# Wider temporaries, an A step's normalisation on ScalarE, and its scores as one scheduling group, in a two-layer hybrid encoder

## The chip, the cores and the metric

The kernel runs on one core of one Trainium2 chip. The metric is the device time of one execution in microseconds (us). A core has a matmul engine (TensorE, written PE, with its weight loads as PEld), a vector engine (VectorE, DVE), an activation engine (ScalarE, ACT), GpSimd (POOL) and a sync engine (SP), which here only issues transfers. Each runs its own instruction list in order, and semaphores tie the lists together. Operands lie in SBUF, an on-chip memory of 128 partitions; matmul results lie in PSUM.

## The reference

Two layers on 512 tokens of width 1024, in float32. Each layer is:

```
h = RMSNorm(x); proj = h @ w_in                      # 2304 columns: qa ka va qb kb vb
qa, ka, qb, kb: per-head RMSNorm, then rotary
group A (8 q heads, 2 kv heads, dim 64, window +-128, learned sink logit per head):
  scores = qa . ka / 8, masked;  m = max(max(scores), sink);  p = exp(scores - m)
  p = p / (sum(p) + exp(sink - m));                  ya = p @ va
group B (4 heads, two q/k halves, values of dim 128):
  w = softmax(s0) - lam * softmax(s1);               yb = rmsnorm(w @ vb) * (1 - lam0)
x = x + concat(ya, yb) @ w_out
h = RMSNorm(x); gate, val = split(h @ w_up)          # 2 x 2816 columns
x = x + (silu(conv3(gate)) * val) @ w_down
```

The change touches group A's line `p = p / (...)`, the moment at which its `scores` are made, and where the tiles lie in SBUF. What is computed stays the same.

## The kernel before, in words

**Matmuls.** Float32 accuracy comes from a split: each operand is a high part (rounded to the matmul's own 32-bit format) and a low part (what is left), and one product is three matmuls (`mm3`, L198 to L200: high·high, high·low, low·high). The second operand of a call, `b` in `mm3`, is the one that streams through the array (the moving operand); the first is loaded as weights. Weights arrive by DMA in units of `wr`; ACT makes the high part `wh` (L185), and DVE or, for the B projections and the output projection, POOL makes the low part `wl` (L186).

**Stages of a layer.** (1) Projection of A's k, v and q (`akv`, `aq0`, `aq1`), the hidden state as weights and 256 weight columns as moving operand. (2) A woven region: attention on one track and, on the other, B's projections (`bv`, `bq`, `bk`, twice) and then the output projection (`wo`). Attention is eight A steps (four query blocks for each of two head pairs, `ip`) and then the B steps. (3) The tail of the output projection. (4) The channel mixer in two parts: `up` (in all 704 triples of 128x512 matmuls with the normed hidden state `nf_h`/`nf_l` moving) and `dn` (352 triples with `act`, the gated activation, moving).

**An A step.** `a_scores` makes the scores of two head groups in a two-bank PSUM tile `sc_a` (L425), adds the mask and takes the maxima on DVE (L429, into `so_a` and `mx_a`), and does this a second time for the other two heads. Small DVE operations on 128x4 tiles follow (L438 to L442), four exponentials on ACT with row sums (L447), a sum and a reciprocal on DVE (L450, L452), and four multiplications of a 128x256 or 128x384 tile by the reciprocal of its row (L454, on DVE). In the next step's turn `a_values` transposes the four tiles on PE (`pt_a`, L470), splits them into high and low parts `p_a` on ACT and DVE (L251, L252) and multiplies by the values (`pv_a`).

**Order.** The two tracks are generators. `weave` always advances the track that is behind in the weights its steps yield. That sets the order in which the code is written out, and thereby the priority of each instruction; a list scheduler with a model of the engines' times then makes each engine's list, and picks by priority among what its model says is ready. Code under `tc.high_priority()` gets priorities as if it stood at the program's start.

**Where tiles lie.** A pool lays its tiles one behind the other in each partition, each rounded up to 32 bytes. Of the eight `tmp` slots each is as long as its longest tile, the 514 floats of `gp` (2056 bytes, rounded to 2080, which is 32 over a multiple of 64). `cols`, `rows` and three one-float constants also add odd multiples of 32. As a sum of these, the tiles of the tags `keep`, `pair`, `prob` and `rp` start 32 bytes past a multiple of 64: among them `act`, the output projection's `y`, `p_a`, A's and B's k and q. The tiles of `hid` (`nf_h`, `nf_l` and the hidden state of the projections), `wr`, `wh`, `wl` and `x` start at a multiple of 64.

Of the kernel before, what the change touches and what calls it, by code (L numbers as in the profile page):

```python
# [21 lines left out]
DEPTH = 2  # L22
HD = 64
# [14 lines left out]
N_COL = NK + NK + 3 * NF + NF + 1  # L38
N_ROW = 4 * HD + 8 + 4 * HD
# [3 lines left out]
def kernel(  # L43
# [16 lines left out]
    nc = tc.nc  # L60
    PSUM = bass.MemoryType.PSUM

    const = ctx.enter_context(tc.tile_pool(name="const", bufs=1))
    sb = ctx.enter_context(tc.tile_pool(name="sb", bufs=1))
# [12 lines left out]
        return sb.tile([P, 2, S], F32R, tag="prob", bufs=4, name=name)  # L77

    def tmp(name, n=S):
        return sb.tile([P, n], F32, tag="tmp", bufs=8, name=name)  # L80

    def rp(name):
        return sb.tile([P, 2, CW], F32, tag="rp", bufs=RP, name=name)
# [1 line left out]
    def small(name, n):  # L85
        return sb.tile([P, n], F32, tag="small", bufs=28, name=name)
# [10 lines left out]
    def sc2(name):  # L97
        return ps.tile([P, 2, S], F32, tag="sc", bufs=1, name=name)
# [40 lines left out]
    x_v = xT.rearrange("(k p) s -> p k s", p=P)  # L139
    out_v = out.rearrange("(k p) s -> p k s", p=P)  # L140
    ident = const.tile([P, P], F32, name="ident")
    cols = const.tile([P, DEPTH, N_COL], F32, name="cols")
    rope_sb = const.tile([P, 2, NT, HD], F32, name="rope_sb")
    mask_sb = const.tile([P, 3 * P], F32, name="mask_sb")
    ones = const.tile([P, 1], F32, name="ones")
    nhalf = const.tile([P, 1], F32, name="nhalf")
    nc.gpsimd.memset(ones, 1.0)
    nc.gpsimd.memset(nhalf, -0.5)

# [53 lines left out]
    class Norm:  # L203
# [47 lines left out]
        nc.scalar.copy(hi, src)  # L251
        nc.vector.tensor_tensor(out=lo, in0=src, in1=hi, op=ALU.subtract)  # L252

    warm = const.tile([P, 1], F32, name="warm")
    nc.scalar.activation(warm, ones, AF.Copy, scale=ones)
    nc.sync.dma_start(cols, col_par)
    nc.sync.dma_start(x_sb[0], x_v[:, 0])
    emit_unit()
    for k in range(1, NK):
# [12 lines left out]
    for l in range(depth):  # L272
        lam_init = 0.8 - 0.6 * math.exp(-0.3 * l)

        rows = sb.tile([P, N_ROW], F32, tag="rows", bufs=1, name=f"rows{l}")
        nc.sync.dma_start(rows, row_par[l:l + 1, :].partition_broadcast(P))
        tabs = [None] * 4

# [13 lines left out]
        if l:  # L292
# [14 lines left out]
                                op0=ALU.subtract, op1=ALU.subtract)  # L307
# [103 lines left out]
        def a_scores(ip, qb):  # L411
            kb0, kb1 = max(qb - 1, 0), min(qb + 2, NT)
            n = (kb1 - kb0) * P
            m0 = (kb0 - qb + 1) * P
            nm = f"a{l}_{ip}_{qb}"
            q, k = qa[ip], ka
            mx = small(f"mx_{nm}", 4)
            so = []
            for i in range(2):
                scp = sc2(f"sc_{nm}_{i}")  # L420
                sc = (scp[:, 0], scp[:, 1])
                for j, (u, v) in enumerate(((0, 0), (0, 1), (1, 0))):
                    for g in range(2):
                        rs = slice(g * HD, (g + 1) * HD)
                        nc.tensor.matmul(sc[g][:, :n], lhsT=q[u][rs, i, qb * P:(qb + 1) * P],  # L425
                                         rhs=k[v][rs, kb0 * P:kb1 * P], start=j == 0, stop=j == 2)
                for g in range(2):
                    s = tmp(f"so_{nm}_{i}_{g}")
                    nc.vector.tensor_tensor_reduce(out=s[:, :n], in0=sc[g][:, :n], in1=mask_sb[:, m0:m0 + n],  # L429
                                                   op0=ALU.add, op1=ALU.max, scale=1.0, scalar=-3.0e38,  # L430
                                                   accum_out=mx[:, 2 * i + g:2 * i + g + 1])
                    so.append(s)
                yield 1.0
            by_g = lambda v: v.rearrange("p (g i) -> p i g", g=2)[:, 2 * ip:2 * ip + 2, :]
            pairs = lambda v: v.rearrange("p (i g) -> p i g", g=2)
            rq = rqa[:, qb, 2 * ip:2 * ip + 2, :]
            ngm = small(f"ng_{nm}", 4)
            nc.vector.tensor_tensor(out=pairs(mx), in0=pairs(mx), in1=rq, op=ALU.mult)  # L438
            nc.vector.scalar_tensor_tensor(out=pairs(ngm), in0=pairs(mx), scalar=-1.0, in1=by_g(nsink),
                                           op0=ALU.mult, op1=ALU.min)  # L440
            dn = small(f"dn_{nm}", 4)
            nc.vector.tensor_tensor(out=pairs(dn), in0=pairs(ngm), in1=by_g(sink), op=ALU.add)  # L442
            es = small(f"es_{nm}", 4)
            nc.scalar.activation(es, dn, AF.Exp)
            ls = small(f"ls_{nm}", 4)
            for i in range(4):
                nc.scalar.activation(so[i][:, :n], so[i][:, :n], AF.Exp, bias=ngm[:, i:i + 1],  # L447
                                     scale=rqa[:, qb, 2 * ip + i // 2, i % 2:i % 2 + 1],
                                     accum_out=ls[:, i:i + 1])
            nc.vector.tensor_tensor(out=ls, in0=ls, in1=es, op=ALU.add)  # L450
            rl = small(f"rl_{nm}", 4)
            nc.vector.reciprocal(rl, ls)  # L452
            for i in range(4):
                nc.vector.tensor_scalar(out=so[i][:, :n], in0=so[i][:, :n], scalar1=rl[:, i:i + 1], scalar2=None,  # L454
                                        op0=ALU.mult)
            a_so[ip, qb] = so

        def a_values(ip, qb):
# [134 lines left out]
        def attend():  # L593
# [104 lines left out]
        for pi, (f0, f1) in enumerate(FF_PARTS):  # L698
            act = []
            for f in range(f0, f1):  # L700
# [7 lines left out]
                g = tmp(f"gp{l}_{f}", S + 2)  # L708
# [103 lines left out]
```

## Time and profile before

| | |
|---|---|
| median of 3 runs (lowest to highest) | 1294.73 us (1293.69 to 1295.14) |
| the profiled execution: its time | 1294.65 us |
| its span on the core | 1292.9 us |
| mean granted TensorE clock | 0.977 of full speed |
| PE busy in the span | 1239.9 us (96%) |
| DVE, ACT, POOL busy | 754.8, 541.8, 359.6 us |
| woven region's A part, layer 0 and layer 1 | about 65 to 190 us and 690 to 820 us |
| woven region's later part | about 190 to 300 us and 820 to 935 us |

The page shows one execution. A line of its table of groups gives, for all instructions of one line of code, engine and operation: output and inputs, their shapes, how often, the busy time, the mean duration in ns, and the idle time of the engine ahead of them with what ended most of it. A timeline row gives start and length in us, engine, line, operation and, in brackets, how long the engine had stood idle and who ended that. A row of the table of windows gives, for a stretch, its length, each engine's busy time with the number of instructions, the granted clock, the DMA share and GB/s. In the profile a matmul's duration is longer than its distance to the next one, because matmuls overlap: the rate is read from one start to the next. The mask operation at L429 is shown under its custom name.

### The profile page before, as it was taken

How to read it: one execution, taken by the hardware profiler on the slowest of the kernel's cores; microseconds unless marked ns; L12 is line 12 of the kernel's file. 1: busy time of each engine (PE TensorE's matmuls, PEld its weight loads, DVE VectorE, ACT ScalarE, POOL GpSimd, SP SyncE). 2: the span in 40 equal slices, each digit the busy share in tenths (PEclk: the TensorE clock that was granted, in tenths of full speed). 3: DMA queues.
4: the chain of work that ended last, by engine and by line, in shares of the span. 5: the costliest groups of instructions: out<-in, count | busy, mean ns of one | idle time of the engine just before them, and what ended most of it. 6: DMA issues, size and time to landing. Idle time of an engine off the chain costs nothing. (4 is left out here: it accounts for less than half of the span.)

```text
span 1292.9 us, 17021 instructions
## 1 busy us (share of the span) xinstructions
PE 1239.9 (96%) x6648; PEld 1040.6 (80%) x6648; DVE 754.8 (58%) x1245; ACT 541.8 (42%) x943; POOL 359.6 (28%) x354
## 2 busy tenths in 40 slices
PE   6999997989999999999999999888999999999998
PEld 6988885778888888888899889766888888888886
DVE  6678787766755334554446778756765542355532
ACT  4455564435433213333345666444443331233321
POOL 5746283114111000112247556602321110011100
PEclk8999999899999999999999999969999999999999
DMA  5312121013332333332332111201233323333232
GB/s 174 99 34 66 42 65 34 26 40 103 96 96 87 96 94 114 97 93 72 98 98 81 51 36 64 65 1 34 65 99 113 96 76 98 106 98 98 80 108 90
DMA packets 32625, 102.93 MB, mean 80 GB/s; under 512 B 3616, under 2 KB 4000, under 8 KB 32544
## 3 DMA queue, kind: packets, MB, share of 16 engines
q1 hardware_dynamic: 32544, 101.84, 25.9%
q8 instruction: 52, 0.85, 0.3%
q14 instruction: 29, 0.24, 0.1%
HBM read 99.73 MB, written 2.10 MB: 79 GB/s over the span
## 5 line engine op out<-in xcount | busy, mean ns | idle before, releaser
L185 ACT CAST wh<-wr 128x1024 fp32r<-128x1024 f32 (+3 forms) x210 | 197.5, 944 | 408.6 <-PE up L199 171.0
L199 PE MATMUL up<-nf_l,wh 128*128 128x512 f32 x704 | 274.7, 390 | 0.6 <-DVE nf_l L217 0.5
L200 PE MATMUL up<-nf_h,wl 128*128 128x512 f32 x704 | 274.1, 390 | 0.4
L198 PE MATMUL up<-nf_h,wh 128*128 128x512 f32 x704 | 273.4, 390 | 0.0
L186 DVE TENSOR_TENSOR wl<-wr,wh 128x1024 fp32r<-128x1024 f32 (+3 forms) x174 | 192.5, 1110 | 108.7 <-ACT wh L185 108.4
L718 POOL TENSOR_TENSOR cv<-cv,rb 128x512 f32<-128x512 f32 x44 | 59.2, 1346 | 519.3 <-ACT cv L717 519.3
L199 PEld LDWEIGHTS up<-nf_l,wh 128*128 128x128 f32 x704 | 132.2, 188 | 29.8 <-DVE nf_l L217 2.8
L200 PEld LDWEIGHTS up<-nf_h,wl 128*128 128x128 f32 x704 | 132.2, 188 | 28.8 <-DVE wl L186 1.5
L198 PEld LDWEIGHTS up<-nf_h,wh 128*128 128x128 f32 x704 | 132.2, 188 | 27.5 <-ACT nf_h L216 0.2
L200 PE MATMUL dn<-act,wl 128*128 128x512 f32 x352 | 139.5, 397 | 0.0
L199 PE MATMUL dn<-act,wh 128*128 128x512 f32 x352 | 139.4, 397 | 0.0
L198 PE MATMUL dn<-act,wh 128*128 128x512 f32 x352 | 138.8, 395 | 0.0
L186 POOL TENSOR_TENSOR wl<-wr,wh 128x1024 fp32r<-128x1024 f32 x36 | 86.9, 2419 | 106.4 <-ACT wh L185 106.4
L711 DVE TENSOR_TENSOR gp<-up,rb 128x512 f32<-128x512 f32 x44 | 30.3, 693 | 103.4 <-PE up L200 98.4
L199 PEld LDWEIGHTS dn<-act,wh 128*128 128x128 f32 x352 | 66.8, 190 | 16.5
L198 PEld LDWEIGHTS dn<-act,wh 128*128 128x128 f32 x352 | 66.0, 188 | 16.5
L200 PEld LDWEIGHTS dn<-act,wl 128*128 128x128 f32 x352 | 66.1, 188 | 15.5
L719 DVE TENSOR_TENSOR cv<-cv,up 128x512 f32<-128x512 f32 x44 | 30.2, 687 | 81.8 <-POOL cv L718 72.1
L522 ACT ACTIVATE e_b<-sc_b,mx_b,rqb 128x512 f32<-128x512 f32 x64 | 49.2, 773 | 49.5 <-DVE mx_b L519 45.6
L732 DVE TENSOR_TENSOR x<-x,dn 128x512 f32<-128x512 f32 x32 | 22.0, 689 | 79.7 <-PE dn L200 79.7
L717 ACT ACTIVATE cv<-cv 128x512 f32<-128x512 f32 x44 | 27.7, 631 | 71.6 <-DVE cv L716 71.5
L518 DVE TENSOR_REDUCE mx_b<-sc_b 128x2 f32<-128x1024 f32 x32 | 39.0, 1219 | 7.9 <-PE sc_b L516 7.8
(212 smaller groups left out, 2559.9 us busy)
## 6 DMA issues: line engine op xcount, KB each, us to landing
wr<-w_up SPq DMA_DIRECT2D x88, 512.0 KB, 3.6
wr<-w_in SPq DMA_DIRECT2D x36, 512.0 KB, 3.6
wr<-w_down SPq DMA_DIRECT2D x32, 384.0 KB, 3.0
wr<-w_down SPq DMA_DIRECT2D x32, 320.0 KB, 2.9
wr<-w_out SPq DMA_DIRECT2D x16, 512.0 KB, 3.6
x<-xT SPq DMA_DIRECT2D x8, 256.0 KB, 5.3
outT<-x SPq DMA_DIRECT2D x8, 256.0 KB, 2.0
rows<-row_par SPq DMA_DIRECT2D x2, 260.0 KB, 4.2
```

The lines of the kernel that those rows point to most:

```text
L185: nc.scalar.copy(hi[:, o], raw[:, o])
L186: eng.tensor_tensor(out=lo[:, o], in0=raw[:, o], in1=hi[:, o], op=ALU.subtract)
L198: nc.tensor.matmul(acc, lhsT=a[0], rhs=b[0], start=start, stop=False)
L199: nc.tensor.matmul(acc, lhsT=a[0], rhs=b[1], start=False, stop=False)
L200: nc.tensor.matmul(acc, lhsT=a[1], rhs=b[0], start=False, stop=stop)
L518: nc.vector.tensor_reduce(out=mx, in_=scp, axis=AX, op=ALU.max)
L522: nc.scalar.activation(e[c], sc[c], AF.Exp, bias=mx[:, c:c + 1], scale=rq[:, c:c + 1], accum_out=lsum[:, c:c + 1])
L711: nc.vector.tensor_tensor(out=g[:, 1:S + 1], in0=acc[0], in1=rb, op=ALU.mult)
L717: nc.scalar.activation(cv, cv, AF.Silu)
L718: nc.gpsimd.tensor_tensor(out=cv, in0=cv, in1=rb, op=ALU.mult)
L719: nc.vector.tensor_tensor(out=cv, in0=cv, in1=acc[1], op=ALU.mult)
L732: nc.vector.tensor_tensor(out=x_sb[d], in0=x_sb[d], in1=acc, op=ALU.add)
```

## The change

It has three parts.

1. Tiles are made wider: a `tmp` tile has 528 floats and is used through a view of its first columns; `cols` and `rows` get 7 and 8 spare columns; the three one-float constants become columns of one 16-float tile. All tiles but the `small` and `smp` ones then start at a multiple of 64 bytes. The DMA into `cols` now writes two stretches of 105 floats in each partition, where it was one of 210.
2. The 64 multiplications at L454 (four in each of 16 A steps) move from DVE to ACT, as an activation `Copy` with the reciprocal as scale.
3. The two halves of an A step's scores (12 matmuls) and their four mask-and-maximum operations stand under `tc.high_priority()`, and the generator yields once, 2.0, instead of twice 1.0.

```diff
     def tmp(name, n=S):
-        return sb.tile([P, n], F32, tag="tmp", bufs=8, name=name)
+        return sb.tile([P, S + 16], F32, tag="tmp", bufs=8, name=name)[:, :n]
...
-    cols = const.tile([P, DEPTH, N_COL], F32, name="cols")
+    cols = const.tile([P, DEPTH, N_COL + 7], F32, name="cols")
...
-    ones = const.tile([P, 1], F32, name="ones")
-    nhalf = const.tile([P, 1], F32, name="nhalf")
+    unit = const.tile([P, 16], F32, name="unit")
+    ones, nhalf, warm = (unit[:, i:i + 1] for i in range(3))
...
-    warm = const.tile([P, 1], F32, name="warm")
     nc.scalar.activation(warm, ones, AF.Copy, scale=ones)
-    nc.sync.dma_start(cols, col_par)
+    nc.sync.dma_start(cols[:, :, :N_COL], col_par)
...
-        rows = sb.tile([P, N_ROW], F32, tag="rows", bufs=1, name=f"rows{l}")
+        rows = sb.tile([P, N_ROW + 8], F32, tag="rows", bufs=1, name=f"rows{l}")[:, :N_ROW]
...
-            for i in range(2):
-                scp = sc2(f"sc_{nm}_{i}")
...
-                yield 1.0
+            with tc.high_priority():
+                for i in range(2):
+                    scp = sc2(f"sc_{nm}_{i}")
...
+            yield 2.0
...
             for i in range(4):
-                nc.vector.tensor_scalar(out=so[i][:, :n], in0=so[i][:, :n], scalar1=rl[:, i:i + 1], scalar2=None,
-                                        op0=ALU.mult)
+                nc.scalar.activation(so[i][:, :n], so[i][:, :n], AF.Copy, scale=rl[:, i:i + 1])
             a_so[ip, qb] = so
```

Past L254 the lines of the changed kernel have numbers smaller by one up to the A step's scores; L454 is L454 in both. The order of SP's list is the same in both. PE's list differs only in the A parts of the two woven regions and just ahead of them; the lists of the B steps, the output projection and the channel mixer have the same order.

On DVE, in layer 0, between the reciprocal of one A step (`rl_a_0_2`, head pair 0, query block 2) and the split of its last transposed block (`p_a_0_1_2` is the step before), the list before is this (the last numbers of a name are buffer numbers):

```order
L450 TENSOR_TENSOR ls_a_0_2_940<-ls_a_0_2_940,es_a_0_2_938 128x4
L452 RECIPROCAL rl_a_0_2_946<-ls_a_0_2_940 128x4
L429 ISA so_a_0_3_0_0_1052,mx_a_0_3_1044<-sc_a_0_3_0_1045,mask_sb 128x256
L429 ISA mx_a_0_3_1044 128x1
L429 ISA so_a_0_3_0_1_1054,mx_a_0_3_1044<-sc_a_0_3_0_1045,mask_sb 128x256
L429 ISA mx_a_0_3_1044 128x1
L454 TENSOR_SCALAR so_a_0_2_0_0_906<-so_a_0_2_0_0_906,rl_a_0_2_946 128x384
L454 TENSOR_SCALAR so_a_0_2_0_1_908<-so_a_0_2_0_1_908,rl_a_0_2_946 128x384
L454 TENSOR_SCALAR so_a_0_2_1_0_929<-so_a_0_2_1_0_929,rl_a_0_2_946 128x384
L454 TENSOR_SCALAR so_a_0_2_1_1_931<-so_a_0_2_1_1_931,rl_a_0_2_946 128x384
L252 TENSOR_TENSOR p_a_0_1_2_991<-pt_a_0_1_2_986,p_a_0_1_2_991 128x512
```

and now this:

```order
L450 TENSOR_TENSOR ls_a_0_2_938<-ls_a_0_2_938,es_a_0_2_936 128x4
L452 RECIPROCAL rl_a_0_2_944<-ls_a_0_2_938 128x4
L429 ISA so_a_0_3_0_0_1050,mx_a_0_3_1042<-sc_a_0_3_0_1043,mask_sb 128x256
L429 ISA mx_a_0_3_1042 128x1
L429 ISA so_a_0_3_0_1_1052,mx_a_0_3_1042<-sc_a_0_3_0_1043,mask_sb 128x256
L429 ISA mx_a_0_3_1042 128x1
L252 TENSOR_TENSOR p_a_0_1_2_989<-pt_a_0_1_2_984,p_a_0_1_2_989 128x512
L429 ISA so_a_0_3_1_0_1061,mx_a_0_3_1042<-sc_a_0_3_1_1054,mask_sb 128x256
```

The four multiplications are gone from DVE's list, and the split follows the masks at once.

On ACT at the same place, between the last exponential of that step and the projection's scaled copy `raw_bq`, before:

```order
L447 ACTIVATE so_a_0_2_1_1_931,ls_a_0_2_940<-so_a_0_2_1_1_931,ng_a_0_2_933,rqa_377 128x384
L251 CAST p_a_0_1_2_991<-pt_a_0_1_2_986 128x512
L185 CAST wh_995<-wr_994 128x1024
L185 CAST wh_1001<-wr_1000 128x1024
L333 ACTIVATE raw_bq_1_1230<-pj_bq_1_1148,na_r 128x256 x2
```

and now:

```order
L447 ACTIVATE so_a_0_2_1_1_917,ls_a_0_2_938<-so_a_0_2_1_1_917,ng_a_0_2_931,rqa_375 128x384
L251 CAST p_a_0_1_2_989<-pt_a_0_1_2_984 128x512
L185 CAST wh_993<-wr_992 128x1024
L454 ACTIVATE so_a_0_2_0_0_904<-so_a_0_2_0_0_904,rl_a_0_2_944 128x384
L454 ACTIVATE so_a_0_2_0_1_906<-so_a_0_2_0_1_906,rl_a_0_2_944 128x384
L454 ACTIVATE so_a_0_2_1_0_915<-so_a_0_2_1_0_915,rl_a_0_2_944 128x384
L454 ACTIVATE so_a_0_2_1_1_917<-so_a_0_2_1_1_917,rl_a_0_2_944 128x384
L185 CAST wh_999<-wr_998 128x1024
L332 ACTIVATE raw_bq_1_1239<-pj_bq_1_1146,na_r 128x256 x2
```

The four multiplications stand behind one conversion of weights `wh` and ahead of the next.

On PE, at the start of layer 1's A part (the last bank of the projection `aq1`, whose transposes are `tr_qa_1`, and the first A step's scores), before:

```order
L371 MATMUL tr_qa_1_6027<-ident,raw_qa_1_6013 128x128 x4
L198 MATMUL pj_aq_1_6116<-wh_5883,na_h_5617 128x256
L199 MATMUL pj_aq_1_6116<-wl_5884,na_h_5617 128x256
L200 MATMUL pj_aq_1_6116<-wh_5883,na_l_5618 128x256
L198 MATMUL pj_aq_1_6116<-wh_5883,na_h_5668 128x256
L199 MATMUL pj_aq_1_6116<-wl_5884,na_h_5668 128x256
L200 MATMUL pj_aq_1_6116<-wh_5883,na_l_5669 128x256
L425 MATMUL sc_a_0_0_0_6192<-ka_5718,qah_0_5878 128x256 x4
L425 MATMUL sc_a_0_0_0_6192<-ka_5718,qal_0_5879 128x256 x2
L198 MATMUL pj_bv_0_6219<-wh_5889,na_h_5319 128x256
```

and now:

```order
L198 MATMUL pj_aq_1_6114<-wh_5725,na_h_5317 128x256
L425 MATMUL sc_a_0_0_0_6190<-ka_5716,qah_0_5876 128x256 x4
L199 MATMUL pj_aq_1_6114<-wl_5726,na_h_5317 128x256
L200 MATMUL pj_aq_1_6114<-wh_5725,na_l_5318 128x256
L198 MATMUL pj_aq_1_6114<-wh_5725,na_h_5365 128x256
L425 MATMUL sc_a_0_0_0_6190<-ka_5716,qal_0_5877 128x256 x2
L199 MATMUL pj_aq_1_6114<-wl_5726,na_h_5365 128x256
L200 MATMUL pj_aq_1_6114<-wh_5725,na_l_5366 128x256
```

The first scores have moved ahead of the projection's last bank. In the whole program, the PE work that lies between the second half of a step's scores and that step's first transpose has become longer in some steps and shorter in others; counted in 256-column matmuls and their like, the shortest of the sixteen is about an eighth shorter than the shortest before.

More of the change, by code (lines that the diff above doesn't have):

```diff
@@ L418, in a_scores @@
             so = []
-            for i in range(2):
-                scp = sc2(f"sc_{nm}_{i}")
-                sc = (scp[:, 0], scp[:, 1])
-                for j, (u, v) in enumerate(((0, 0), (0, 1), (1, 0))):
-                    for g in range(2):
[L424 to L432, printed above, removed]
-                yield 1.0
+            with tc.high_priority():
+                for i in range(2):
+                    scp = sc2(f"sc_{nm}_{i}")
+                    sc = (scp[:, 0], scp[:, 1])
+                    for j, (u, v) in enumerate(((0, 0), (0, 1), (1, 0))):
+                        for g in range(2):
+                            rs = slice(g * HD, (g + 1) * HD)
+                            nc.tensor.matmul(sc[g][:, :n], lhsT=q[u][rs, i, qb * P:(qb + 1) * P],
+                                             rhs=k[v][rs, kb0 * P:kb1 * P], start=j == 0, stop=j == 2)
+                    for g in range(2):
+                        s = tmp(f"so_{nm}_{i}_{g}")
+                        nc.vector.tensor_tensor_reduce(out=s[:, :n], in0=sc[g][:, :n], in1=mask_sb[:, m0:m0 + n],
+                                                       op0=ALU.add, op1=ALU.max, scale=1.0, scalar=-3.0e38,
+                                                       accum_out=mx[:, 2 * i + g:2 * i + g + 1])
+                        so.append(s)
+            yield 2.0
             by_g = lambda v: v.rearrange("p (g i) -> p i g", g=2)[:, 2 * ip:2 * ip + 2, :]
```

## The prediction

> **What bounds the kernel now.** I read the page first: the busy shares and the slices.
>
> ```profile
> span 1292.9 us, 17021 instructions
> PE 1239.9 (96%) x6648; PEld 1040.6 (80%) x6648; DVE 754.8 (58%) x1245; ACT 541.8 (42%) x943; POOL 359.6 (28%) x354
> PE   6999997989999999999999999888999999999998
> PEclk8999999899999999999999999969999999999999
> ```
>
> PE is busy for 96% of the span, and the slices with less are the start and the two woven regions (a slice is 32.3 us; the dips stand at the second to ninth and the 26th to 29th). So there are two ways to gain: make PE's matmuls themselves shorter, or remove its pauses in the woven regions. The change tries both. The windows tell the channel mixer and the woven regions apart.
>
> ```profile
> 360.00:370.00 10.00, 10.00 (x46) 8.29 (x45) 4.92 (x7) 4.10 (x5) 1.36 (x3) 1.00 0.33 105
> 440.00:450.00 10.00, 10.00 (x44) 8.02 (x43) 3.68 (x5) 1.82 (x3) 0.00 (x0) 1.00 0.26 79
> 65.00:190.00 125.00, 117.48 (x844) 102.97 (x843) 96.04 (x221) 75.21 (x178) 68.68 (x49) 0.97 0.16 49
> 190.00:300.00 110.00, 96.63 (x541) 76.74 (x541) 81.61 (x136) 50.95 (x99) 33.93 (x21) 0.94 0.14 43
> 690.00:820.00 130.00, 127.99 (x945) 113.89 (x944) 98.54 (x238) 81.03 (x186) 79.92 (x54) 0.99 0.19 54
> ```
>
> In the mixer (360 is `up`, 440 is `dn`) PE never pauses, at full clock: every nanosecond off a matmul there is a nanosecond off the total. In layer 0's A part PE is idle for 7.5 of 125 us, in layer 1's for 2.0 of 130; the later parts are idle for more (13.4 of 110), but the change leaves their order as it is. In the A parts DVE has the most to do beside PE, ACT some 20 us less.
>
> **Part 1, the padding.** The two mixer windows differ: 46 matmuls started in 10 us of `up`, 44 in 10 us of `dn`, though both are 128x512 matmuls. The timeline gives the rate.
>
> ```profile
> 359.68 0.39 PE L200 MATMUL up<-nf_h,wl 128*128 128x512 f32 x1
> ...
> 362.85 0.39 PE L199 MATMUL up<-nf_l,wh 128*128 128x512 f32 x1
> ```
>
> ```profile
> 439.81 0.40 PE L200 MATMUL dn<-act,wl 128*128 128x512 f32 x1
> ...
> 442.86 0.40 PE L198 MATMUL dn<-act,wh 128*128 128x512 f32 x1
> ```
>
> ```profile
> 191.68 0.40 PE L199 MATMUL wo<-yl,wh 128*128 128x512 f32 x1
> ...
> 194.25 0.39 PE L198 MATMUL wo<-yh,wh 128*128 128x512 f32 x1
> ```
>
> From the first to the last row quoted there are 14 starts of `up` (3.17 us, 226.4 ns each), 13 of `dn` (3.05 us, 234.6 ns) and 11 of `wo` (2.57 us, 233.6 ns). What sets the slow two apart is where the moving tile starts: `act` and `y` 32 bytes past a multiple of 64, `nf` at a multiple. The excess is the same for two stages with different stationary tiles and different neighbours, and `dn` runs with DVE and ACT nearly idle, so I put it on the address. It is an inference: no row of before has the same tile at both places. After the padding I take both to run at 226.4 ns.
>
> ```profile
> L200 PE MATMUL dn<-act,wl 128*128 128x512 f32 x352 | 139.5, 397 | 0.0
> L198 PE MATMUL wo<-yh,wh 128*128 128x512 f32 x64 | 26.2, 410 | 0.0
> L198 PE MATMUL wo<-yh_b,wh 128*128 128x512 f32 x32 | 13.7, 429 | 0.0
> L198 PE MATMUL pv_a<-p_a,va 128*128 128x512 f32 x40 | 16.9, 421 | 0.0
> ```
>
> `dn`: 3 x 352 = 1056 matmuls by 8.2 ns = 8.7 us, all on the path that sets the end. `wo` (without its last, half-wide pass): 3 x 96 = 288 by 7.2 ns = 2.1 us; these fill the woven regions' later parts, where PE waits on attention 12% of the time, and filler that gets shorter there turns partly into waiting, so I count half, 1.0. `pv_a`: 3 x 40 = 120 by the same 7 ns = 0.8 us, and the B scores, whose keys also lie at the odd place, some 1 us more; half of both is 0.8. Sum of the padding: -8.7 - 1.0 - 0.8 = **-10.5 us**. Bounds: 0 if the address is not the cause, and -12.6 if all of these (8.7 + 2.1 + 0.8 + 1.0) count in full.
>
> The Trainium skill speaks against this part: "SBUF — State Buffer", Specifications (TRN2), gives SBUF cachelines of 16 bytes and a penalty for each step to a new line. By that rule a tile that starts 32 bytes past a multiple of 64 starts on a line as much as one at 64, the padding does nothing, and the rows above would need another cause.
>
> The DMA into `cols` has twice the pieces of half the length and stands first in the program; I count 0.1 us at most, and nothing in the sum. The other edits of this part change no instruction's size.
>
> **Part 2, the multiplications.** On DVE they cost this:
>
> ```profile
> L454 DVE TENSOR_SCALAR so_a<-so_a,rl_a 128x384 f32<-128x384 f32 x32 | 22.0, 751 | 0.0
> L454 DVE TENSOR_SCALAR so_a<-so_a,rl_a 128x256 f32<-128x256 f32 x32 | 18.0, 622 | 0.0
> 70.52 5.18 DVE L454 TENSOR_SCALAR so_a<-so_a,rl_a 128x256 f32<-128x256 f32 x4
> 83.13 1.41 DVE L454 TENSOR_SCALAR so_a<-so_a,rl_a 128x384 f32<-128x384 f32 x4
> ```
>
> Four usually take 1.41 us, but 5.18 at 70.52 (and of the smaller size). At that moment POOL runs the low part of weights, and PE stands:
>
> ```profile
> 70.28 4.75 POOL L186 TENSOR_TENSOR wl<-wr,wh 128x1024 fp32r<-128x1024 f32 x2 [2.44 <-ACT wh L185]
> 75.50 1.02 PE L470 MATMUL pt_a<-ident,so_a 128*128 128x128 f32 x6 [2.17 <-DVE so_a L454]
> 101.40 0.33 PE L470 MATMUL pt_a<-ident,so_a 128*128 128x128 f32 x1 [1.98 <-DVE so_a L454]
> 144.58 0.66 PE L470 MATMUL pt_a<-ident,so_a 128*128 128x128 f32 x4 [1.19 <-DVE p_a L252]
> 151.36 0.30 PE L470 MATMUL pt_a<-ident,so_a 128*128 128x128 f32 x1 [1.17 <-DVE so_a L454]
> 754.67 0.66 PE L470 MATMUL pt_a<-ident,so_a 128*128 128x128 f32 x4 [2.01 <-DVE so_a L454]
> ```
>
> POOL's two operations cover 70.28 to 75.03, the multiplications end at 75.70, and the transposes that wait for the last of them start just then. So a two-input POOL operation holds up DVE's multiplication, and PE pays 2.17 us. Four pauses of PE are of this kind: 2.17 + 1.98 + 1.17 + 2.01 = 7.3 us. The fifth (1.19) waits for a DVE split and stays. Three of them are followed by a lower clock:
>
> ```profile
> 70.00:80.00 10.00, 7.69 (x50) 6.71 (x50) 9.45 (x19) 4.94 (x12) 4.75 (x2) 0.83 0.36 107
> 100.00:110.00 10.00, 8.33 (x53) 7.59 (x54) 7.29 (x18) 4.77 (x14) 6.74 (x6) 0.83 0.32 95
> 750.00:760.00 10.00, 7.99 (x54) 7.37 (x53) 9.41 (x18) 4.37 (x11) 7.57 (x6) 0.83 0.36 106
> ```
>
> A mean clock of 0.83 over 10 us is 1.7 us of matmul lost, three times 5.1. Together 7.3 + 5.1 = 12.4 us hang on the multiplications.
>
> On ACT no such operation stands in the trace; it is bounded by these:
>
> ```profile
> L216 ACT ACTIVATE nf_h<-x,cols 128x512 fp32r<-128x512 f32 x16 | 10.5, 712 | 8.2 <-DVE x L667 8.2
> L185 ACT CAST wh<-wr 128x1024 fp32r<-128x1024 f32 x138 | 144.8, 1050 | 235.8 <-PE up L199 146.7 <-issue 32.5 <-PE dn L199 26.0
> L185 ACT CAST wh<-wr 128x768 fp32r<-128x768 f32 x32 | 26.8, 837 | 98.1 <-PE dn L199 86.0 <-PE up L199 12.1
> ```
>
> The first is the same operation, a copy with a per-partition scale, at 512 columns. The casts give the slope, (1050 - 837) / 256 = 0.83 ns a column. So 384 columns cost 712 - 107 = 606 ns and 256 cost 499: four take 2.4 or 2.0 us, against 1.4 on a DVE that is left alone. In all ACT gains 32 x 0.606 + 32 x 0.499 = 35 us, about 18 in each A part, and reaches some 75 + 18 = 93 us of 125; DVE loses 40 us in all. Neither becomes the busiest. What gets longer is one step's chain, by about 1 us with 384 columns, and more where a `wh` cast of 1.05 us stands ahead of the multiplications on ACT's queue, as the list shows; behind them stands the cast of `p_a` and the next `wh`, for which PE's next matmuls wait. ACT shows no operation that POOL holds up (the casts at L185 keep their 1050 ns on the mean).
>
> The Trainium skill, "ScalarE: Activation LUTs", Rules for kernel authors, says to keep a multiplication on VectorE, since it is faster there per element. The trace agrees for an undisturbed one (1.41 us for four against 2.4), and not for a disturbed one (5.18).
>
> **Part 3, the group.** It adds no instruction. It moves scores ahead; what counts is the PE work between a step's second scores and its first transposes. That is a little shorter at its shortest, about 8 us where it was 9, while the chain it must cover (masks, small operations, four exponentials, sum, reciprocal, four multiplications) is 1 us longer. Some steps will still leave PE waiting. I take 60% of the 12.4 us as gained, for parts 2 and 3 together: **-7.5 us**. Bounds: -12.4, and 0 (or worse, below).
>
> **Sum.** The profiled execution took 1294.65 us (1.75 of them outside its span), and the median of the runs is 1294.73: one base. 1294.65 - 10.5 - 7.5 = 1276.65, say **1276.7 us**.
>
> **The rivals.**
> - All the pauses go: 1294.65 - 10.5 - 12.4 = 1271.8. For it: ACT has 50 us of slack in the first A part. Against it: the longer chain, and DVE's small two-input operations that POOL can still hold up (the 144.58 row is one).
> - The pauses only move, from "waits for DVE's multiplication" to "waits for ACT's" or to the fifth row's kind, and the A parts gain nothing: 1294.65 - 10.5 = 1284.2. For it: the chain is 1 us longer and its cover 1 us shorter.
> - The address is not what slows `dn`, and the padding does nothing: 1294.65 - 7.5 = 1287.2. This is the case that the skill's rule of 16-byte lines would make. For it: nothing in the trace varies the address alone. Against it: three stages sort by address without exception.
> - Both of these: no change, about 1294.
> - Slower: ACT's queue becomes the A step's bound. A step whose multiplications stand behind a cast leaves PE idle for 2 us, and if the clock falls after it, 1.7 more: 3.7 a step. Against it stand 12.4 + 10.5 = 22.9 us of gains, so it decides from seven of the sixteen steps on; with eight it is 8 x 3.7 - 22.9 = +6.7, 1301.4. Against it: ACT is busy for only 60% of the A part.
>
> **How the numbers follow.** Forecast 0.50, all pauses gone 0.10, pauses moved 0.20, no effect of the address 0.11, neither 0.05, slower 0.04. Within 0.2% (2.6 us, about what a measurement of this kernel can tell from no change) lies the "neither" case alone: 0.05. Faster gets 0.50 + 0.10 + 0.20 + 0.11 = 0.91, slower 0.04. The range goes from 1270 (all pauses gone, with the padding counted in full: 1294.65 - 12.6 - 12.4 = 1269.7) to 1289 (no effect of the address, with somewhat less gained from the pauses); this leaves out the last two cases and tails of the others.
>
> **What would show it.** Right: starts of `dn` 226 ns apart, and 46 of them in 10 us; no L454 on DVE, and on ACT at 0.6 and 0.5 us; PE's waits for `so_a` shorter than 7.3 us in sum, and fewer windows at 0.83 of the clock in the A parts. Wrong: `dn` still at 234 ns (the address is not it); waits of `pt_a` for ACT of 2 us each with a low clock behind them (the pauses moved); or a wait in the later parts that takes back what `wo` gained.

## The result

The changed kernel takes 1282.64 us in the median of four runs (1280.52 to 1283.72), against 1294.24 for the kernel before beside it: a ratio of 0.9905, 95% interval 0.9892 to 0.9917, 12 us or 0.95% faster. The forecast was 1276.7 with a range of 1270 to 1289: the way and the range held, the time came 6 us later. Its profiled execution took 1282.14 us. First the page, with the rows that answer to those of before:

```profile
span 1280.4 us, 17034 instructions
PE 1226.6 (96%) x6648; PEld 1034.8 (81%) x6648; DVE 737.5 (58%) x1181; ACT 569.6 (44%) x1007; POOL 359.2 (28%) x354
PE   6999996989999999999999999978999999999998
PEclk8999998899999999999999999979999999999999
```

DVE has 64 instructions fewer and ACT 64 more, as the change says. The clock still dips below nine tenths early in layer 0, now in the seventh slice and not the eighth, and rose from 6 to 7 tenths in the 27th. The windows, at the places looked at before:

```profile
70.00:80.00 10.00, 10.00 (x78) 8.96 (x78) 6.01 (x15) 7.67 (x19) 4.79 (x2) 1.00 0.36 107
100.00:110.00 10.00, 10.00 (x78) 9.21 (x78) 6.99 (x19) 6.81 (x16) 8.93 (x8) 1.00 0.02 9
750.00:760.00 10.00, 10.00 (x81) 9.35 (x79) 8.23 (x16) 7.92 (x19) 7.56 (x7) 1.00 0.38 107
65.00:190.00 125.00, 120.59 (x879) 106.01 (x877) 88.79 (x195) 91.03 (x212) 75.21 (x54) 1.00 0.18 54
190.00:300.00 110.00, 93.36 (x512) 74.52 (x511) 77.12 (x130) 49.45 (x97) 28.36 (x17) 0.89 0.13 39
440.00:450.00 10.00, 10.00 (x45) 8.15 (x44) 2.55 (x3) 1.78 (x3) 0.00 (x0) 1.00 0.37 116
```

The three windows with a clock of 0.83 are full now. Layer 0's A part has 4.4 us of idle PE, not 7.5, at full clock. But the part behind it has 16.6 idle, not 13.4, and its clock fell from 0.94 to 0.89. And `dn` has 45 starts in 10 us, neither the 44 of before nor the 46 that were forecast. The timeline gives its rate:

```profile
439.80 0.39 PE L199 MATMUL dn<-act,wh 128*128 128x512 f32 x1
440.03 0.40 PE L200 MATMUL dn<-act,wl 128*128 128x512 f32 x1
440.27 0.39 PE L198 MATMUL dn<-act,wh 128*128 128x512 f32 x1
...
443.25 0.39 PE L199 MATMUL dn<-act,wh 128*128 128x512 f32 x1
```

Counting the rows left out, 15 starts in 3.45 us: 230.0 ns, where 234.6 stood and 226.4 was forecast. The distances aren't even, and repeat every two triples; over all starts of `dn` their mean went from 234.4 to 230.1.

Where the 12.5 us between the two profiled spans come from, by the first and last matmul of each stretch on PE:

| stretch | before, us | changed, us | difference |
|---|---|---|---|
| start to layer 0's first `up` | 288.3 | 286.8 | -1.5 |
| channel mixer, layer 0 (to the end of `dn`) | 366.9 | 364.6 | -2.3 |
| layer 1 to its first `up` | 263.3 | 256.8 | -6.5 |
| channel mixer, layer 1 | 370.7 | 368.4 | -2.2 |

The mixer's -4.5 is `dn` alone: its four passes took 67.68, 56.39, 67.68 and 56.39 us and now take 66.42, 55.41, 66.41 and 55.41. Layer 0 is the puzzle: three of the four pauses stood there, and it gained only 1.5 us. The waits of PE in layer 0's A part, 55 to 190 us:

```profile
PE pv_a L199 <- DVE p_a L252: 1.0, 1, 1.0
PE pv_a L198 <- DVE yl L252: 0.8, 1, 0.8
PE pt_a L469 <- ACT so_a L454: 0.7, 1, 0.7
PE sc_a L425 <- DVE mx_a L429: 0.6, 1, 0.6
PE pj_bk L199 <- POOL wl L186: 0.6, 1, 0.6
PE pj_bq L198 <- ACT raw_bq L332: 0.5, 1, 0.5
```

One wait for a multiplication is left, 0.7 us where there were 5.3; in its place stand five smaller ones of other kinds, among them one of scores for the masks ahead of them.

Layer 1 is a second puzzle: it gained 6.5 us, and PE waits no less there. Its waits in the A part (680 to 815 us; before it was one of 2.0 us), and two windows, first of the kernel before, then of the changed one:

```profile
PE pt_a L469 <- DVE p_a L252: 1.9, 2, 1.5
PE pt_a L469 <- ACT so_a L454: 1.2, 1, 1.2
PE yb L199 <- DVE wl_b L252: 0.6, 1, 0.6
```

```profile
680.00:795.00 115.00, 112.99 (x855) 102.18 (x853) 83.20 (x218) 70.28 (x163) 66.67 (x44) 0.99 0.19 56
795.00:925.00 130.00, 115.45 (x669) 93.84 (x668) 92.01 (x159) 59.31 (x120) 43.93 (x30) 0.89 0.14 41
```

```profile
680.00:795.00 115.00, 111.93 (x864) 101.33 (x863) 81.18 (x192) 86.30 (x203) 66.13 (x45) 1.00 0.17 51
795.00:925.00 130.00, 115.09 (x669) 93.51 (x669) 96.75 (x155) 60.81 (x119) 50.17 (x33) 0.93 0.16 48
```

In the two windows together PE is idle for 16.6 us before and for 18.0 now. What rose is the granted clock, most of it behind the A part: 0.04 of 130 us and 0.01 of 115 are, by estimate, some 6 us. Why the clock stands higher there was not found.

### The profile page after: what moved, and what is told of

The parts are those of the page before. It is cut to its first block, busy times and chain, and to the rows that moved or that the text cites. A ratio compares the mean times of both kernels' runs of the same rounds, so it can differ in the third digit from the quotient of the medians.

```text
span 1280.4 us, 17034 instructions
## 1 busy us (share of the span) xinstructions
PE 1226.6 (96%) x6648; PEld 1034.8 (81%) x6648; DVE 737.5 (58%) x1181; ACT 569.6 (44%) x1007; POOL 359.2 (28%) x354
## 5 line engine op out<-in xcount | busy, mean ns | idle before, releaser
L198 PE MATMUL dn<-act,wh 128*128 128x512 f32 x352 | 137.4, 391 | 0.0
L199 PE MATMUL dn<-act,wh 128*128 128x512 f32 x352 | 137.0, 390 | 0.0
L200 PEld LDWEIGHTS dn<-act,wl 128*128 128x128 f32 x352 | 66.1, 188 | 14.5
```

What stands on the lines that cost most here:

```text
L198: nc.tensor.matmul(acc, lhsT=a[0], rhs=b[0], start=start, stop=False)
L199: nc.tensor.matmul(acc, lhsT=a[0], rhs=b[1], start=False, stop=False)
L200: nc.tensor.matmul(acc, lhsT=a[1], rhs=b[0], start=False, stop=stop)
```

## The experiments

**What sets `dn`'s rate.** The first run adds matmuls behind the changed kernel's end, to read the rate by the start address alone.

```diff
+    def point(name, moves, loads, n):
+        acc = (mm, at)[len(name) % 2](name)[:, :n]
+        for i in range(24):
+            nc.tensor.matmul(acc, lhsT=loads[i % len(loads)], rhs=moves[i % len(moves)], start=i == 0, stop=i == 23)
...
+    for j in range(32):
+        point("qm" + L26[j // 8] + L26[j % 8], [odd[:, 4 * j:4 * j + S]], kk, S)
+    for j in range(16):
+        point("qw" + L26[j], [odd[:, 16:16 + S]], [wf[0][:, 8 * j:8 * j + P]], S)
```

> The changed kernel with 1,400 matmuls added behind its end (their results go nowhere, the output is the same). Each point is 24 matmuls in a row with one moving tile of 128x512 whose start is shifted by 16 bytes from point to point (32 points over 512 bytes), then 16 points with the weights' start shifted by 32 bytes, 4 points with 256 columns, and 4 with the sequence of moving tiles that dn has. Theory A (only the moving tile's start modulo 64 counts): the points at 0, 64, 128, ... bytes run at 226 to 227 ns from start to start, all others at 234 or more, and dn's sequence at 226 as well, so that dn's 230 ns in the changed kernel would come from something else than addresses. Theory B (the moving tile's start counts against that of the weights, which is 64 past a multiple of 512, as it is for the hidden state in up): 226 to 227 only where the moving tile starts at the same remainder as the weights, between 228 and 236 at the others, and shifting the weights moves the rate as well. Theory C (lines of 16 bytes, no further effect): all 32 points alike.

The kernel took 1582.6 us with it. `odd` is an `act` tile that starts at a multiple of 256; `kk` are four weight tiles that start 64 past one. The groups of some points (names end in the step: `qmab` is 16 bytes, `qmad` 48, `qmae` 64, `qmag` 96, `qmba` 128; in the `qw` points the moving tile stays at 64 and the weights move on from 64, `qwa` by 0, `qwc` by 64, `qwg` by 192, `qwi` by 256 bytes):

```profile
L752 PE MATMUL qmab<-act,wh 128*128 128x512 f32 x24 | 5.8, 397 | 0.0
L752 PE MATMUL qmad<-act,wh 128*128 128x512 f32 x24 | 5.6, 388 | 0.0
L752 PE MATMUL qmae<-act,wh 128*128 128x512 f32 x24 | 5.6, 390 | 0.0
L752 PE MATMUL qmag<-act,wh 128*128 128x512 f32 x24 | 5.8, 395 | 0.0
L752 PE MATMUL qmba<-act,wh 128*128 128x512 f32 x24 | 5.7, 392 | 0.0
L752 PE MATMUL qwc<-act,wh 128*128 128x512 f32 x24 | 5.8, 396 | 0.0
L752 PE MATMUL qwg<-act,wh 128*128 128x512 f32 x24 | 5.7, 392 | 0.0
L752 PE MATMUL qwi<-act,wh 128*128 128x512 f32 x24 | 5.6, 389 | 0.0
```

The mean duration differs by about as much as the distance between starts does, and the clock was 1.00 throughout. The mean distances, worked from the starts (the second 256 bytes repeat the first to 0.5 ns, so one period is shown):

| moving tile's start, modulo 256 | 0 | 16 | 32 | 48 | 64 | 80 | 96 | 112 |
|---|---|---|---|---|---|---|---|---|
| ns from start to start | 233.3 | 234.8 | 233.1 | 227.0 | 228.3 | 231.4 | 233.5 | 233.1 |

| moving tile's start, modulo 256 | 128 | 144 | 160 | 176 | 192 | 208 | 224 | 240 |
|---|---|---|---|---|---|---|---|---|
| ns from start to start | 229.3 | 230.9 | 233.7 | 231.1 | 232.8 | 233.4 | 233.8 | 233.2 |

(At 64 the first eight are uneven and the rest run at 226 to 227. `wo`, whose series are at most 22 long, shows the same when its tiles lie at 64, in the kernels further below, and so has less of the gain.) So the multiples of 64 are not alike: 233.3, 228.3, 229.3 and 232.8. Moving the weights does the same as moving the tile: weights at 64 + 64 against a tile at 64 give 233.5, as does a tile at 0 against weights at 64; weights at 64 + 192 give 229.3, as a tile at 128 does; weights at 64 + 256 give 226.7. (Weights at 64 + 0 came first in that series: its first eleven distances are uneven, 230.4 on the mean of all, and the rest run at 226 to 227.) What counts is the start of the moving tile against that of the weights, modulo 256 bytes. Theory A falls and C with it; B stands, but for the start at 48, which is as good as the one at 64. It also comes within 1.2 ns of both kernels: before, `act` lay at 96 and at 224 (two tags, alternating), 233.5 and 233.8; in the changed kernel it lies at 128 and at 0, 229.3 and 233.3, mean 231.3, and `dn` takes 230.1. Three more points ran `dn`'s own order of operands: 233.4 ns on one tag, 229.3 on the other, and 230.6 with the two in turn. `nf` lies at 64, as all weights do, and `up` takes 227. The four points with 256 columns (starts at 0, 32, 64 and 96) run at 118 to 120 ns, and 64 is the slowest of them.

One point doesn't fit: a tile that alternates between 0 and 64 runs at 226.9 ns, not at the mean of its two rates. The order of the starts matters too, and by what rule these runs don't tell.

The Trainium skill, "SBUF — State Buffer", Specifications (TRN2), knows lines of 16 bytes and nothing of a place against the weights; by that rule these points would be alike. They aren't, and the measurement decides.

Two kernels then place the tiles without touching any list. This is the first (tiles at 64 modulo 256); the second has `N_ROW + 40` (tiles at 0):

```diff
-        rows = sb.tile([P, N_ROW + 8], F32, tag="rows", bufs=1, name=f"rows{l}")[:, :N_ROW]
+        rows = sb.tile([P, N_ROW + 56], F32, tag="rows", bufs=1, name=f"rows{l}")[:, :N_ROW]
...
-        rqb = sb.tile([P, NT, 4, 2], F32, tag="rqb", bufs=1, name=f"rqb{l}")
+        rqb = sb.tile([P, NT + 4, 4, 2], F32, tag="rqb", bufs=1, name=f"rqb{l}")[:, :NT]
```

> The changed kernel with spare columns in rows and rqb, so that act, y, k, q, v and p_a start 64 bytes past a multiple of 256, as all weight tiles do; the order of every engine's list is unchanged. If the moving tile's start against the weights' start, modulo 256, sets the rate: dn at 226 to 227 ns from start to start, 3.6 us less than the changed kernel (1056 x 3.4 ns), wo some 2 ns less each, in all 1278 to 1279.5. If a multiple of 64 was all that counts: dn at 230, 1282.6.

> The changed kernel with the same tiles at a multiple of 256, all still multiples of 64, and 64 bytes short of the weights' remainder; lists unchanged. If the start against the weights counts: dn at 233 to 234 ns, 3.5 us more than the changed kernel, 1285 to 1287, and so the padding to 64 bytes undone in dn without an odd address. If a multiple of 64 is what counts: dn at 230 or 226, 1282.6 or less.

The groups of `dn`, first with the tiles at 64, then at 0:

```profile
L200 PE MATMUL dn<-act,wl 128*128 128x512 f32 x352 | 136.6, 389 | 0.0
```

```profile
L200 PE MATMUL dn<-act,wl 128*128 128x512 f32 x352 | 138.4, 394 | 0.0
```

From start to start that is 226.7 and 233.3 ns. The times are 1280.93 us (0.9896, 0.9881 to 0.9911) and 1287.05 (0.9949, 0.9936 to 0.9961), with 1294.6 before: 6.1 us apart, where `dn` alone differs by 7.0. With every tile at a multiple of 64 `dn` can be nearly as slow as before. Against the changed kernel's ratio of 0.9905 the better place is worth less than the 3.6 us that `dn` shows (some 1.2 us, with intervals that overlap); in the profiled executions the stretches ahead of the first `up` are 1.3 and 1.6 us longer than in the changed kernel.

The placement alone, on the kernel before, with `tmp` tiles and constants left as they were:

```diff
-        rows = sb.tile([P, N_ROW], F32, tag="rows", bufs=1, name=f"rows{l}")
+        rows = sb.tile([P, N_ROW + 56], F32, tag="rows", bufs=1, name=f"rows{l}")[:, :N_ROW]
...
-        rqb = sb.tile([P, NT, 4, 2], F32, tag="rqb", bufs=1, name=f"rqb{l}")
+        rqb = sb.tile([P, NT + 4, 4, 2], F32, tag="rqb", bufs=1, name=f"rqb{l}")[:, :NT]
```

> The kernel before with spare columns in rows and rqb alone, so that act, y, k, q, v and p_a start 64 past a multiple of 256 as the weights do; tmp tiles, cols and the constants stay unpadded, and every engine's list stays as before. If the place against the weights is all there is to the padding: dn at 226.7 ns, 8.1 us less (1056 x 7.7 ns), and wo and pv_a a little: 1285 to 1287. If dn's gain is eaten by what follows, as the padding alone looked (4.5 less in dn, 2.2 in all): 1290 or more.

1285.84 us, ratio 0.9935 (0.9921 to 0.9948): 9.1 us by the medians, 8.4 by the ratio, from 352 spare bytes in each partition (56 columns of `rows`, 32 of `rqb`). `dn`, at 226.7 ns, gives 8.1 of them, and every engine's list is as before.

**The change's padding alone** (its lines as in the diff above, the other two parts left out).

> The kernel before with the padding alone. If the padding acts on matmuls only, dn takes 121.8 + 121.8 us as in the changed kernel (4.5 us less in all), wo and pv_a give at most 1 more, and the A parts keep their pauses (7.3 us of waits for L454 and three stretches of low clock): 1288 to 1290. If the padding is what gave the whole gain: about 1282.6. If the gain is not the padding's: 1294.

1292.35 us, ratio 0.9984 (0.9975 to 0.9994), less than expected. `dn` has its 4.5 us (230.1 ns), so the rest of the kernel, with the same lists, gave about half of it back. In the profiled execution that was layer 0's later part. The same window as before:

```profile
190.00:300.00 110.00, 96.50 (x533) 77.25 (x532) 79.68 (x136) 51.45 (x99) 32.06 (x20) 0.91 0.13 39
```

As much idle PE as before (13.5 us), but the clock is 0.91, not 0.94, and layer 0's first `up` starts at 290.7 us, 2.3 later. The lists are the same, so it is a matter of when the pauses fall and what clock is granted after them. These are one execution of each kernel, and single executions of the kernel before differ too (mean clocks from 0.973 to 0.984); what decides it was not found.

**The multiplications alone**, on the kernel before:

```diff
-                nc.vector.tensor_scalar(out=so[i][:, :n], in0=so[i][:, :n], scalar1=rl[:, i:i + 1], scalar2=None,
-                                        op0=ALU.mult)
+                nc.scalar.activation(so[i][:, :n], so[i][:, :n], AF.Copy, scale=rl[:, i:i + 1])
```

> The kernel before with the 64 multiplications on ScalarE alone. Theory: the waits of the transposes for the multiplications fall from 7.3 us to under 3, the clock stays full in both A parts, about 8 us are gained there, and the later part of layer 0 gives back up to half of it: 1287 to 1291. Rival, the pauses only move: 1293 to 1296. Rival, ScalarE's queue is too long without the earlier scores: over 1297.

1283.33 us, ratio 0.9918 (0.9898 to 0.9938): 10.7 us, more than any of the theories gave it. PE's waits in layer 0's A part (55 to 190 us), and its first 115 us as a window:

```profile
PE pj_bq L198 <- ACT raw_bq L333: 0.5, 1, 0.5
PE pt_a L469 <- ACT so_a L454: 0.5, 1, 0.5
```

```profile
55.00:170.00 115.00, 113.95 (x868) 102.18 (x868) 77.83 (x197) 88.36 (x209) 70.96 (x50) 1.00 0.19 58
```

PE is idle for 1.05 us of 115 there, at full clock. Without the group almost all of layer 0's pauses go, and the wait for the multiplications on ScalarE that might have replaced them is 0.5 us. In layer 1's A part the pauses do move: the one of 2.0 us is gone, and three others (1.4, 1.0 and 0.7 us, for VectorE) have come.

**Both parts without the padding** (the changed kernel, with the padding's lines as before).

> The changed kernel without its padding (multiplications on ScalarE and the scores as a group). If the parts add up and the padding is worth 4.5 to 5.5 us: 1287 to 1288. If the padding is worth nothing beside them: 1282.6. If the order gave nothing: 1294.

1288.06 us, ratio 0.9951 (0.9932 to 0.997). The padding is worth 5.6 us beside the other two, as expected. (Not all of that need be addresses: without the padding the lists of PE, DVE and ACT also differ at some places in the B steps.) But this kernel is the one above plus the group, and it is 4.7 us slower than that one, on the same chip: the group costs.

**The group alone**, on the kernel before:

```diff
-            for i in range(2):
-                scp = sc2(f"sc_{nm}_{i}")
+            with tc.high_priority():
+                for i in range(2):
+                    scp = sc2(f"sc_{nm}_{i}")
...
-                yield 1.0
+            yield 2.0
```

> The kernel before with the scores of an A step as one high-priority group, multiplications left on VectorE. If the group costs by itself what it costs beside the multiplications on ScalarE (1288.1 against 1283.3): 1297 to 1300, with the loss in the A parts. If it only costs beside the moved multiplications, since ScalarE's queue is what it disturbs: 1293 to 1295. If it gains where the chain is shorter, as on VectorE: under 1292.

1304.2 us, ratio 1.0074 (1.0055 to 1.0092): slower than any of the theories had it. PE's waits in layer 1's A part, 680 to 815 us, where the kernel before has 2.0 us in all:

```profile
PE pt_a L471 <- DVE p_a L252: 6.7, 2, 3.7
PE pt_a L471 <- DVE so_a L455: 3.0, 2, 2.2
PE sc_a L426 <- DVE mx_a L430: 1.2, 1, 1.2
```

and DVE there, just ahead of one of the long ones:

```profile
764.80 0.18 DVE L453 RECIPROCAL rl_a<-ls_a 128x4 f32<-128x4 f32 x1
764.89 0.53 DVE L430 CUSTOM_DVE_ANT_0 so_a<-sc_a,mask_sb 128x384 f32<-128x384 f32 x1
...
765.82 5.62 DVE L455 TENSOR_SCALAR so_a<-so_a,rl_a 128x384 f32<-128x384 f32 x4
771.36 0.68 DVE L252 TENSOR_TENSOR p_a<-pt_a,p_a 128x512 fp32r<-128x512 f32 x1
```

The four multiplications are held up here too (5.62 us), and the split for which PE waits stands behind them. Which pauses appear depends on how DVE's and POOL's lists happen to meet. With the priority alone and the two yields as before, the lists come out as with the group, so it is the priority that moves them; why they then meet worse was not taken further.

**The change without the group**, and the changed kernel again beside it:

```diff
-            with tc.high_priority():
-                for i in range(2):
...
-            yield 2.0
+            for i in range(2):
...
+                yield 1.0
```

> The changed kernel without the scores' group: padding and multiplications on ScalarE, two yields of 1.0 and no high priority. If the group costs beside the other two parts what the runs so far give (1288.1 - 1283.3 = 4.8 without padding, 1280.9 - 1276.3 = 4.6 with the placement): 1277 to 1279, with the difference in layer 0's A part and the part behind it. If the group's price hung on those two pairs by chance: 1281 to 1283, as the changed kernel.

> The changed kernel once more, on the same chip as the two others, for the difference to the one without the group: 1282 to 1283, 4 to 5 more than that one if the group costs, the same if it doesn't.

1279.27 us (0.9883, 0.9868 to 0.9898) and 1282.39 (0.9911, 0.9896 to 0.9926): 3.1 us, somewhat less than expected. In three pairs that differ by the group beside ScalarE's multiplications it cost 4.7, 4.6 (next run) and 3.1 us. The two layers don't agree, though. In the profiled executions, in us, without the group and with it:

| pair | layer 0: start to first `up` | layer 1: end of `dn` to first `up` |
|---|---|---|
| without padding | 278.4, 288.9 | 260.8, 257.6 |
| with the change's padding | 281.3, 286.4 | 260.8, 256.7 |
| with the tiles at 64 (next run) | 278.1, 288.1 | 261.4, 258.4 |

The group costs 5 to 11 us in layer 0 and gives 3 to 4 in layer 1. (These are single executions, so the sums differ from the medians above.)

**The best of the parts**: the change without the group, with the tiles at 64 modulo 256 by the two widened tiles.

```diff
+        rows = sb.tile([P, N_ROW + 56], F32, tag="rows", bufs=1, name=f"rows{l}")[:, :N_ROW]
+        rqb = sb.tile([P, NT + 4, 4, 2], F32, tag="rqb", bufs=1, name=f"rqb{l}")[:, :NT]
```

> The kernel before with the multiplications on ScalarE and the tiles placed as in the run above that has the weights' remainder of 64 modulo 256, without the scores' group. If the parts add up: ScalarE alone took 10.7 us off, the placement takes 8.2 off dn and 1 to 2 off wo and pv_a: 1294.2 - 10.7 - 9.5 = 1274, between 1272 and 1277. If the group is needed beside the padding: 1278 or more.

1276.29 us, ratio 0.9861 (0.9843 to 0.9879), faster than both kernels; expected was 1274. Its difference to the same placement with the group shows where in layer 0 the group costs. Layer 0's A part and the part behind it, first with the group, then without:

```profile
58.00:170.00 112.00, 107.56 (x816) 95.93 (x817) 77.57 (x192) 83.69 (x199) 67.66 (x47) 1.00 0.20 60
170.00:290.00 120.00, 102.87 (x600) 82.97 (x597) 84.61 (x146) 52.46 (x105) 34.08 (x22) 0.91 0.12 36
```

```profile
58.00:170.00 112.00, 110.89 (x844) 99.48 (x845) 75.01 (x195) 85.65 (x203) 68.94 (x49) 1.00 0.20 60
170.00:290.00 120.00, 105.47 (x604) 84.27 (x603) 86.93 (x147) 57.74 (x110) 41.67 (x25) 0.94 0.14 44
```

With the group PE is idle for 4.4 us in the A part, without it for 1.1; behind it for 17.1 and 14.5, and at a lower clock with the group. That is the puzzle of layer 0: what the multiplications gave there, the group took back. Layer 1's gain is the other half: of the 6.5 us the multiplications alone gave 2.5 and the group most of the rest.

## Why the prediction was right and wrong

**What bounds the kernel: right.** The mixer's rate and the woven regions' pauses are what moved; all of the gain lies in `dn` and in the two stretches ahead of the first `up`. Not foreseen was that the parts behind the A parts move as well. The prediction took their order as unchanged, but PE's order is the same again only from some 220 us on in layer 0 and 845 in layer 1, so the first B steps are in another order too; and the granted clock there, which no term covered, moved the time by some us in both directions.

**Part 1, the padding, -10.5: the step that failed.** It read three stages, saw that the fast one starts at a multiple of 64 and the slow ones don't, and took the rate of the fast one for all. That the address slows `dn` was right; "a multiple of 64" was not the rule. The place against the weights, modulo 256, is: 226.7 ns at the weights' own remainder, 233.3 at another multiple of 64. The padding moved `act` from two slow places to a middling and a slow one, and `dn` got 4.5 us in place of 8.7. The three stages could not tell the two rules apart, since the only fast one has both properties; the prediction said that no row has the same tile at both places, and yet gave the inference the full rate. The bounds (0 to -12.6) did hold it. The 1.8 us for `wo`, `pv_a` and the B scores are not to be seen: `wo`'s middle distance fell from 234 to 231 ns, but the later parts wait on attention anyway. The padding as a whole measured -2.1 alone (0.16% by its ratio), -4.5 beside the multiplications (ratios 0.9918 and 0.9883) and -5.6 beside both parts, where -10.5 was forecast: most of the 6 us by which the time came later.

**Part 2, the multiplications: mechanism right in layer 0, size too small.** POOL's two-input operation held up DVE's multiplications: in the kernel before, the 52 of the 64 that met no POOL operation took 336 to 418 ns each, and the 12 that did 2.0 us on the mean. Off DVE, the four pauses and the three stretches of low clock are gone. Against the 12.4 us that hung on them the run with this part alone got 10.7, 86%, where 60% was assumed. That sum is in part luck. In its profiled execution layer 0 gained 9.9 us of the 8.7 that hung on it, and layer 1 2.5 of 3.7, there with more idle PE than before (3.1 us against 2.0 in the A part) and a higher clock. ScalarE's price was right; the group and timeline rows of the changed kernel:

```profile
L454 ACT ACTIVATE so_a<-so_a,rl_a 128x256 f32<-128x256 f32 (+1 forms) x64 | 30.8, 555 | 5.3 <-DVE rl_a L452 5.3
```

```profile
90.83 2.13 ACT L454 ACTIVATE so_a<-so_a,rl_a 128x384 f32<-128x384 f32 x4
89.67 1.30 POOL L361 TENSOR_TENSOR raw_bq<-raw_bq,tab 128x512 f32<-128x512 f32 x1
91.04 1.30 POOL L362 TENSOR_TENSOR raw_bq<-raw_bq,sq_bq 128x512 f32<-128x512 f32 x1
```

The mean of both sizes is 555 ns, by the estimate (606 + 499) / 2 = 552; four of the larger ones in a row overlap and take 2.13 us, not 2.4. The rule of the Trainium skill ("ScalarE: Activation LUTs", Rules for kernel authors) that a multiplication belongs on VectorE is a rule about the operation alone, and its figure is for bf16. The Trainium skill, "SBUF — State Buffer", Terms, says that VectorE and GpSimd share a port pair which one of them holds for a whole instruction, and that ScalarE has its own. The runs agree: four multiplications beside POOL's work took up to 5.7 us on DVE, and on ACT, where 31 of the 64 met a POOL operation as in the rows above, none took more than 0.62 us.

**Part 3, the group: wrong sign in sum.** It was counted with part 2 at 60% of 12.4, as something that shortens the cover and leaves some pauses, not as a cost of its own. Alone it costs 9.6 us and loses in both layers; beside the multiplications it costs 3 to 5, as the sum of a loss in layer 0 and a smaller gain in layer 1. What spoke for a cost was there: the PE work between scores and transposes got shorter in some steps. What was missed is that each half's scores can now wait for the masks of the half before (`sc_a` waits 0.6, 0.7 and 1.2 us in three kernels with the group, and nowhere in the A parts before), and that a new order ahead of DVE's splits can open pauses where there were none. These waits are smaller than the cost; how the rest of it comes about, and why layer 1 gains, stays open. Together the parts measured -6.0 (1288.1) where -7.5 was forecast; two errors of 3 to 5 us each nearly cancelled.

**The rivals.** "The pauses only move" came true in a part: five small waits in layer 0's A part, and more idle time at a lower clock behind it. In layer 0 it was the group, not ScalarE's chain, that moved them; in layer 1 the multiplications alone did, to waits for VectorE. "ScalarE's queue becomes the bound" can be excluded: with its 64 more operations alone, PE waits 0.5 us for the multiplications and 0.5 for another ScalarE operation in layer 0's A part, and for none in layer 1's. "The address isn't it" is excluded by the two placements that differ in nothing else.

## What to carry to other kernels

When one stage's matmuls run some ns slower than another's of the same shape, list the start of the moving tile and of the weights for both, and vary the start in a run before naming a rule; here a shift of two tags by some bytes gave 8 to 9 us of 1294. A change of three parts wants three runs: here one of them cost about as much as another gave. And read the result layer by layer: a part that loses in one place and gains in another looks small in the sum. An operation may be dearer on the other engine and still save time, if it leaves an engine that a third one blocks.

## What the runs showed of the hardware that was not expected

- 128x512 matmuls in this 32-bit format start every 226.7 ns when moving tile and weights start at the same remainder of 256 bytes, and up to 234.8 ns (3.6%) at others, tried in steps of 16 bytes; a tile 16 bytes short of the weights' remainder is fast too (227.0). With 256 columns, tried at four starts, no such effect is seen (118 to 120 ns). Why, and why a tile that alternates between two starts runs at the fast rate of 226.9, stays open.
- A per-row multiplication of 128x256 or 128x384 slowed from about 0.4 us to 2.0 on the mean on DVE when POOL worked beside it, and on ACT stayed at 0.49 to 0.62 us.
- With identical lists on all engines the granted clock of a part with pauses differed between two profiled executions (0.94 and 0.91 over the same 110 us). That is worth as much as a small change; whether the padding or chance between executions made it was not separated.
